# Three of the four column blocks of the embedding's product run at the start, around x's transposes, and wait in DRAM

## The chip, the cores and the metric

One program runs on one core of a Trainium2 chip. The metric is the device time of an execution in microseconds (us); the smaller is the better. The time of a kernel is the median over its runs.

## What is computed

One decoder layer over 512 tokens of width 2048 in float32: RMSNorm, one wide input projection, a recurrence over 16 heads and a pooling group, an output projection with a residual, a gated per-layer embedding, and a final RMSNorm. The change touches the first step and the embedding:

```python
h = rms_norm(x, norm_g[i])
z = jnp.einsum('btd,dn->btn', h, w_in[i])
...
x = x + jnp.einsum('btc,cd->btd', y_mix, w_out[i])
gate = jax.nn.sigmoid(jnp.einsum('btd,de->bte', x, w_pg[i]) + b_pg[i])
x = x + gate * jnp.einsum('btq,qd->btd', p[i], w_ple[i])
return rms_norm(x, final_g)
```

Here p is 512 x 256 and w_ple is 256 x 2048. The product p @ w_ple depends on no other result, so it can run at any time before the gates that use it.

## The kernel before, in words

Every matrix product is made of three: each operand is split into a rounded high part (a cast on ScalarE, ACT) and a low part (a subtraction on VectorE, DVE), and `mm3` (L163) issues high x high, high x low and low x high. A 256 KB piece of weights is loaded on SP's DMA queue into `raw`, then split into `whi` and `wlo` (`wsplit`, L127, or `split`, L136); each of the three has a ring of four buffers.

The stages, in time:

- **Start** (L51 to L298). x comes as four row blocks `xt0` to `xt3` of 128 x 2048, 256 KB or 512 KB at a time. `stats` (L233) squares a block on ACT and DVE, sums, takes the root, and scales the block in place in four quarters. `xt_half(hf, d)` (L264) transposes 128 columns of two row blocks on TensorE (PE) into PSUM; ACT writes the high part `hhi` and DVE the low part `hlo`. There are 2 x 16 such pairs. `z_half` (L274) multiplies them with the 128 columns of the small lora weights (`whi_l`, `wlo_l`) into `zl`. The PSUM tiles of the transposes alternate between the pools `psM` and `psX` of three buffers each. The scheduler may order the matmuls of this stage as it likes.
- **Middle** (L301 to L844). 32 column blocks of w_in for the head groups and 16 for the pooling, pinned in program order on PE; the first is `zk`. The recurrence's small matmuls are threaded between them.
- **Output projection** (L927): four column blocks of 512 of w_out, accumulators `acc_o`, residual x2, transposed back for the gate.
- **Gates** (L1015 to L1042): four column blocks of w_pg, accumulators `acc_g`. `proj` (L877) goes over 16 weight pieces k and, within one, over the four row blocks tt, three matmuls each: 192 matmuls a column block. Accumulators rotate through five PSUM buffers, and a block needs four of them. `gate` (L963) is, for each row block, an addition on DVE that empties the accumulator (L973), a tanh on ACT, two more DVE operations (`gt`), a square on ACT and a multiplication into `x3` on DVE.
- **The embedding** (`embed`, L906): p is transposed and split once, late (L846 to L850). For a column block, two pieces of w_ple pass through the weights' rings, 24 matmuls write four PSUM tiles `pple`, and ACT copies them to `ple`. Block 0 runs in the last block of the output projection (L939). Block ec+1 runs on PE between the projections of gate blocks ec and ec+1 (L1020).

Of the kernel before, what the change touches and what calls it, by code (L numbers as in the profile page):

```python
# [34 lines left out]
def trunk_kernel(ctx: ExitStack, tc: tile.TileContext, x, p, norm_g, w_in, mu, w0, w_up, a0, a_up,  # L35
# [20 lines left out]
    def load_x(tt, parts):  # L56
        xt = xp.tile([P, D], F32, name=f"xt{tt}", tag="xt")
        w_ = D // parts
        for i in range(parts):
            nc.sync.dma_start(out=xt[:, i * w_:(i + 1) * w_], in_=x[tt * P:(tt + 1) * P, i * w_:(i + 1) * w_])  # L60
        xs.append(xt)

    load_x(0, 4)
    ngr = xp.tile([KT, P], F32, name="ngr", bufs=1)
    nc.sync.dma_start(out=ngr, in_=norm_g[0].rearrange("(r c) -> r c", c=P))
# [68 lines left out]
        return hi, lo  # L134

    def split(hi, lo, src):  # L136
        nc.scalar.copy(hi, src)  # L137
        nc.vector.tensor_tensor(lo, src, hi.bitcast(F32), ALU.subtract)  # L138


    def rsqrt(y, v, t):
# [72 lines left out]
    def load_l():  # L214
        n_, c_, src, kt, w_ = plan.pop(0)
        raw = wp.tile([P, kt, w_], F32, name=f"raw_{n_}_{c_}", tag="raw")
        nc.sync.dma_start(out=raw, in_=src)
        lraw.append(raw)

    for step in LORD:  # L220
        if step == "l":
            load_l()
        else:
            load_x(step, 2)

# [2 lines left out]
        nc.sync.dma_start(out=prow[col[n_]:col[n_] + r_, :], in_=flat.rearrange("(r c) -> r c", c=P))  # L228


    WPOS, SPOS = (5, 7, 9, 11), (5, 10)

    def stats(tt, parts=2):  # L233
        w_ = D // parts
        ss = xp.tile([P, parts], F32, name=f"ss{tt}", tag="ss")
        for i in range(parts):
            cs = slice(i * w_, (i + 1) * w_)
            junk = xp.tile([P, w_], F32, name=f"junk{tt}_{i}", tag=f"junk{i % 2}", bufs=2)
            if i % 2 == 0:
                nc.scalar.activation(junk, xs[tt][:, cs], AF.Square, accum_out=ss[:, i:i + 1])  # L240
            else:
                nc.vector.scalar_tensor_tensor(junk, xs[tt][:, cs], 1.0, xs[tt][:, cs], ALU.mult, ALU.mult,
                                               accum_out=ss[:, i:i + 1])
        rs = xp.tile([P, 1], F32, name=f"rs{tt}", tag="rs")
        nc.vector.tensor_reduce(rs, ss, mybir.AxisListType.X, ALU.add)
        nc.scalar.activation(rs, rs, AF.Sqrt, bias=epsr, scale=1.0 / D)
        nc.vector.reciprocal(rs, rs)
        for i in range(4):
            cs = slice(i * D // 4, (i + 1) * D // 4)
            if i % 2 == 1:  # L250
                nc.scalar.activation(xs[tt][:, cs], xs[tt][:, cs], AF.Copy, scale=rs)
            else:
                nc.vector.tensor_scalar(xs[tt][:, cs], xs[tt][:, cs], rs, None, ALU.mult)

    stats(0, 4)
    pt = psM.tile([P, T], F32, name="pt_prm", tag="m")
    nc.tensor.transpose(pt[:, :KT], ngr, ident[:KT, :KT])
# [5 lines left out]

    def xt_half(hf, d):  # L264
        hc = half(hf)
        pt = (psM, psX)[d % 2].tile([P, T], F32, name=f"pt_h{hf}_{d}", tag="mx"[d % 2])
        for i in range(2):
            src = xs[2 * hf + i][:, d * P:(d + 1) * P]
            nc.tensor.transpose(pt[:, i * P:(i + 1) * P], src, ident)
        nc.scalar.activation(hhi[:, d, hc], pt[:, 0:256], AF.Copy, scale=ngc[:, d:d + 1])  # L270
        nc.vector.scalar_tensor_tensor(hlo[:, d, hc], pt[:, 0:256], ngc[:, d:d + 1], hhi[:, d, hc].bitcast(F32),
                                       ALU.mult, ALU.subtract)

    def z_half(hf, d):  # L274
        hc = half(hf)
        wh, wl = wl_[d // CK]
        mm3(zl[:, hc], wh[:, d % CK, :], wl[:, d % CK, :], hhi[:, d, hc], hlo[:, d, hc], d == 0, d == KT - 1)

    wl_ = []
    for d in range(KT):  # L280
        xt_half(0, d)
        if d in WPOS:
            c = len(wl_)
            wh = wp.tile([P, CK, P], F32R, name=f"whi_l_{c}", tag="whi")
            wl = wp.tile([P, CK, P], F32R, name=f"wlo_l_{c}", tag="wlo")
            split(wh, wl, lraw[c])
            wl_.append((wh, wl))
        if d in SPOS:
            stats(2 + SPOS.index(d))
# [5 lines left out]
    pt = psM.tile([P, T], F32, name="pt_prm", tag="m")  # L295
    nc.tensor.transpose(pt[:, :nr], prow, ident[:nr, :nr])
    nc.vector.tensor_copy(prm, pt[:, :nr])
    sx.close()  # L298


# [564 lines left out]
    EC = 512  # L865
    KEEP = 8
    TP = 40
    AS = (3,)
# [37 lines left out]
    def embed(ec, pool):  # L906
        es = slice(ec * EC, (ec + 1) * EC)
        src = w_ple[:, es].rearrange("(k p) n -> p k n", p=P)
        ph, pl = [], []
        for k in range(2):  # L910
            a_, b_ = wsplit(src[:, k:k + 1, :], 1, EC, f"ple{ec}_{k}")
            ph.append(a_)
            pl.append(b_)
        ple = []
        for tt in range(NT):
            ts_ = slice(tt * P, (tt + 1) * P)
            pq = psM.tile([P, EC], F32, name=f"pple{ec}_{tt}", tag="m")
            for k in range(2):
                nc.tensor.matmul(pq, phi[:, k, ts_], ph[k][:, 0, :], start=k == 0, stop=False)  # L919
# [3 lines left out]
            nc.scalar.copy(t_, pq)  # L923
# [25 lines left out]
    with tc.tile_pool(name="fp", bufs=2) as fp, tc.tile_pool(name="kp_", bufs=1) as kp_:  # L949
# [115 lines left out]
```

## Time and profile before

| | |
|---|---|
| median of 3 runs | 1123.04 us (1122.91 to 1123.46) |
| the profiled execution's own time | 1124.35 us |
| its span, first to last instruction | 1122.6 us |
| PE, DVE, ACT, POOL busy | 1081.4, 709.3, 459.9, 75.2 us |
| mean granted TensorE clock | 0.993 |
| DMA | 130.17 MB, mean 116 GB/s |

All times in the trace are from the span's start. PE is TensorE's matmuls, DVE VectorE, ACT ScalarE, POOL GpSimd, SP the queue that issues most loads; PEld is the weight load of PE. A row of a timeline gives start, length, engine, line, operation, what it writes and reads, and in brackets the idle time ahead of it with what ended it. Matmuls are pipelined: a 128x512 one is shown as 0.39 us long, but the next starts 0.23 us behind it, so starts and not lengths are to be subtracted.

### The profile page before, as it was taken

What the parts mean: (1) busy time and instruction counts of PE and PEld (TensorE: products, weight loads), DVE (VectorE), ACT (ScalarE), POOL (GpSimd) and SP (SyncE); (2) the same over time, 40 slices, a digit from 0 to 9 for tenths busy, and PEclk for the clock granted to TensorE, in tenths of its full rate; (3) what the DMA queues carried; (4) which work ended last, traced back from release to release, by engine and by line L of the source; (5) the groups of instructions that cost most, each with busy time, mean ns of one, the idle gap of its engine ahead of it and who ended that gap; (6) DMA issues with size and microseconds to landing.
All of it is one profiled execution on the core that took longest, in us unless ns stands there. A gap on an engine that the chain in (4) does not pass through costs nothing. (4 is left out here: it accounts for less than half of the span.)

```text
span 1122.6 us, 17272 instructions
## 1 busy us (share of the span) xinstructions
PE 1081.4 (96%) x6090; PEld 880.6 (78%) x6090; DVE 709.3 (63%) x1861; ACT 459.9 (41%) x920; POOL 75.2 (7%) x184
## 2 busy tenths in 40 slices
PE   5999999999999998999999999999999999999995
PEld 4888887877877876878778787778888888888885
DVE  6677868778588687687885955564243332525446
ACT  7643536336336353363362343252222232424333
POOL 2100010110110100101101102000000000000001
PEclk9999999999999998999999999999999999999998
DMA  7433332423423332324234233465343444434244
GB/s 228 122 92 96 101 105 69 114 85 82 121 78 93 99 77 71 100 74 110 79 89 120 74 104 96 150 215 174 115 161 125 138 145 155 150 104 151 94 132 150
DMA packets 173877, 130.17 MB, mean 116 GB/s; under 512 B 34165, under 2 KB 139230, under 8 KB 173790
## 3 DMA queue, kind: packets, MB, share of 16 engines
q1 hardware_dynamic: 157694, 103.89, 31.6%
q10 hardware_dynamic: 16096, 25.17, 6.9%
q8 instruction: 48, 0.79, 0.3%
q14 instruction: 39, 0.32, 0.1%
HBM read 113.82 MB, written 14.68 MB: 114 GB/s over the span
## 5 line engine op out<-in xcount | busy, mean ns | idle before, releaser
L133 DVE TENSOR_TENSOR wlo_g<-raw_g,whi_g 128x512 fp32r<-128x512 f32 x88 | 59.4, 684 | 78.6 <-ACT whi_g L132 78.4
L156 PE MATMUL zb<-hhi,whi_b 128*128 128x512 f32 x256 | 107.2, 419 | 0.0
L133 DVE TENSOR_TENSOR wlo_o<-raw_o,whi_o 128x512 fp32r<-128x512 f32 x64 | 43.8, 691 | 93.7 <-ACT whi_o L132 93.7
L156 PE MATMUL acc_o<-wlo_o,yhi 128*128 128x512 f32 x256 | 99.9, 390 | 0.6 <-DVE wlo_o L133 0.6
L156 PE MATMUL zb<-hhi,wlo_b 128*128 128x512 f32 x256 | 100.5, 392 | 0.0
L156 PE MATMUL acc_o<-whi_o,ylo 128*128 128x512 f32 x256 | 100.3, 392 | 0.0
L132 ACT CAST whi_g<-raw_g 128x512 fp32r<-128x512 f32 x88 | 54.3, 623 | 112.2 <-PE acc_g L156 62.1
L156 PE MATMUL zb<-hlo,whi_b 128*128 128x512 f32 x256 | 100.0, 391 | 0.0
L156 PE MATMUL acc_o<-whi_o,yhi 128*128 128x512 f32 x256 | 99.4, 391 | 0.5 <-ACT yhi L137 0.5
L156 PE MATMUL acc_g<-whi_g,x2hi 128*128 128x512 f32 x224 | 86.5, 386 | 0.0
L156 PE MATMUL acc_g<-wlo_g,x2hi 128*128 128x512 f32 x224 | 86.4, 386 | 0.0
L156 PE MATMUL acc_g<-whi_g,x2lo 128*128 128x512 f32 x224 | 86.3, 385 | 0.0
L132 ACT CAST whi_o<-raw_o 128x512 fp32r<-128x512 f32 x64 | 39.7, 623 | 101.1 <-PE acc_o L156 93.6
L749 POOL TENSOR_SCALAR s0p<-sbd,pw 64x64 f32<-64x64 f32 x96 | 52.9, 551 | 331.9 <-DVE sbd L742 255.3
L132 ACT CAST whi_b<-raw_b 128x512 fp32r<-128x512 f32 x64 | 39.6, 619 | 73.5 <-PE zv L156 27.7
L133 DVE TENSOR_TENSOR wlo_b<-raw_b,whi_b 128x512 fp32r<-128x512 f32 x64 | 43.8, 685 | 29.0 <-ACT whi_b L132 28.5
L156 PEld LDWEIGHTS acc_o<-wlo_o,yhi 128*128 128x128 f32 x256 | 48.1, 188 | 11.4 <-DVE wlo_o L133 1.5
L156 PEld LDWEIGHTS zb<-hhi,wlo_b 128*128 128x128 f32 x256 | 48.0, 188 | 10.9
L156 PEld LDWEIGHTS acc_o<-whi_o,yhi 128*128 128x128 f32 x256 | 48.1, 188 | 10.5 <-ACT yhi L137 0.7
L156 PEld LDWEIGHTS acc_o<-whi_o,ylo 128*128 128x128 f32 x256 | 48.1, 188 | 10.0 <-DVE ylo L138 0.4
L597 DVE TENSOR_TENSOR xw<-xw,tm 128x60 f32<-128x60 f32 (+24 forms) x248 | 51.9, 209 | 6.3
L156 PEld LDWEIGHTS zb<-hhi,whi_b 128*128 128x128 f32 x256 | 48.3, 189 | 8.7
(290 smaller groups left out, 2568.2 us busy)
## 6 DMA issues: line engine op xcount, KB each, us to landing
raw_b<-in_w_in_dram SPq DMA_DIRECT2D x64, 256.0 KB
raw_o<-in_w_out_dram SPq DMA_DIRECT2D x64, 256.0 KB
raw_g<-in_w_pg_dram SPq DMA_DIRECT2D x64, 256.0 KB
raw_k<-in_w_in_dram SPq DMA_DIRECT2D x32, 256.0 KB
raw_r<-in_w_in_dram SPq DMA_DIRECT2D x32, 256.0 KB
raw_v<-in_w_in_dram SPq DMA_DIRECT2D x32, 256.0 KB
raw_g<-in_w_in_dram SPq DMA_DIRECT2D x32, 256.0 KB
n<-nd SPq DMA_DIRECT2D x16, 256.0 KB
```

What stands on the lines that cost most here:

```text
L132: nc.scalar.copy(hi, raw)
L133: nc.vector.tensor_tensor(lo, raw, hi.bitcast(F32), ALU.subtract)
L156: i = nc.tensor.matmul(*a, **k)
L597: nc.vector.tensor_tensor(xw[:, 0:n_, s + 1:32], xw[:, 0:n_, s + 1:32], tm[:, 0:n_, 0:w_], ALU.add)
L749: nc.gpsimd.tensor_scalar(s0p[hc, :], nxt[hc, hc], pcn[hc], None, ALU.mult)
```

## The change

Column blocks 1, 2 and 3 of the embedding's product move to the start. A generator `embed_early` transposes and splits p, and hands out the 72 matmuls of the three blocks six at a time; results go from PSUM to a tile `pe_` and on ACT's DMA queue to a DRAM tensor `pled`. `recall` loads a block back from there at the place in the gate stage where `embed(ec + 1)` stood. Block 0 stays where it was, and so do the late transposes and splits of p for it, so p is now loaded and transposed twice.

With it come these:

- SP's queue begins with p (`pn0`, 512 KB) and w_ple's block 1 (`eraw`, 512 KB), ahead of x. Block 2 comes after the first half of x, block 3 after all of x and the lora weights, which now follow x.
- At the start PE is pinned in program order: p's transposes, block 1 (24 matmuls), then the pairs of the first half of x with block 2 between them, then `z_half(0)` with the pairs of the second half four steps behind it, then `z_half(1)`, block 3, and `zk`.
- The low parts of the lora weights and of blocks 2 and 3 are subtracted on POOL (`split_g`); the lora splits come later (WPOS).
- x's transposes use three PSUM buffers (`psX`) and no longer six.

```diff
+    EC = 512
...
+    def load_e(ec):
+        for k in range(2):
+            t_ = xp.tile([P, EC], F32, name=f"eraw{ec}_{k}", tag="eraw", bufs=6)
+            nc.sync.dma_start(out=t_, in_=w_ple[k * P:(k + 1) * P, ec * EC:(ec + 1) * EC])
+            eraw[ec, k] = t_
+
+    load_e(1)
     load_x(0, 4)
...
+    def split_g(hi, lo, src):
         nc.scalar.copy(hi, src)
-        nc.vector.tensor_tensor(lo, src, hi.bitcast(F32), ALU.subtract)
+        nc.gpsimd.tensor_tensor(lo, src, hi.bitcast(F32), ALU.subtract)
...
-    LORD = (2, "l", "l", "l", "l", 3)
+    LORD = ("e2", 2, 3, "l", "l", "l", "l", "e3")
...
-    WPOS, SPOS = (5, 7, 9, 11), (5, 10)
+    WPOS, SPOS = (11, 13, 14, 15), (5, 11)
...
+    def embed_early():
+        ph0 = xp.tile([P, 2, T], F32R, name="ph0", bufs=1)
+        pl0 = xp.tile([P, 2, T], F32R, name="pl0", bufs=1)
+        for k in range(2):
+            pt = psM.tile([P, T], F32, name=f"ppt0_{k}", tag="m")
+            for tt in range(NT):
+                tr(pt[:, tt * P:(tt + 1) * P], pn0[tt // 2][:, tt % 2, k * P:(k + 1) * P], ident)
+            first[:] = split(ph0[:, k, :], pl0[:, k, :], pt)
+        yield 0
+        for ec in range(1, D // EC):
+            w2 = []
+            for k in range(2):
...
+                if ec == 1:
+                    split(hi, lo, eraw[ec, k])
+                else:
+                    with tc.issue_after(ev[0].ins):
+                        split_g(hi, lo, eraw[ec, k])
...
+            for tt in range(NT):
+                ts_ = slice(tt * P, (tt + 1) * P)
+                pq = psM.tile([P, EC], F32, name=f"pe{ec}_{tt}", tag="m")
+                for k in range(2):
+                    hi, lo = w2[k]
+                    mm3(pq, ph0[:, k, ts_], pl0[:, k, ts_], hi, lo, k == 0, k == 1)
+                    yield 3
+                t_ = xp.tile([P, EC], F32, name=f"pe_{ec}_{tt}", tag="pe", bufs=4)
+                if ec == 1:
+                    nc.scalar.copy(t_, pq)
+                else:
+                    nc.vector.tensor_copy(t_, pq)
+                nc.scalar.dma_start(out=pled[ts_, ec * EC:(ec + 1) * EC], in_=t_)
...
+    pin[0] = True
...
+    ple(24)
+    with tc.issue_after(first[0].ins), tc.issue_after(first[1].ins):
+        stats(0, 4)
...
     for d in range(KT):
         xt_half(0, d)
+        ple(2 if d > 3 else 0)
         if d in WPOS:
...
-            split(wh, wl, lraw[c])
+            with tc.issue_after(ev[0].ins):
+                split_g(wh, wl, lraw[c])
...
-    for d in range(KT):
-        xt_half(1, d)
-        z_half(0, d)
+    for d in range(KT + 4):
+        if d >= 4:
+            xt_half(1, d - 4)
+        if d < KT:
+            z_half(0, d)
...
     for d in range(KT):
         z_half(1, d)
...
+    ple(100)
+    pin[0] = False
...
+    def recall(ec, pool):
+        ples[ec] = []
+        for tt in range(NT):
+            t_ = pool.tile([P, EC], F32, name=f"ple{ec}_{tt}", tag="ple", bufs=4)
+            nc.scalar.dma_start(out=t_, in_=pled[tt * P:(tt + 1) * P, ec * EC:(ec + 1) * EC])
+            ples[ec].append(t_)
...
-            embed(ec + 1, fp if ec % 2 == 0 else lp)
+            recall(ec + 1, fp if ec % 2 == 0 else lp)
```

The order of instructions on each engine shows what moved at three places. First, PE at the start, before: after the transpose of norm_g (`ngr`) come the transposes of x (`xt`).

```order
L257 MATMUL pt_prm<-ident,ngr 128x16
L269 MATMUL pt_h_0_198<-ident,xt_78 128x128
L269 MATMUL pt_h_1_203<-ident,xt_78 128x128
L269 MATMUL pt_h_2_208<-ident,xt_78 128x128
L269 MATMUL pt_h_3_213<-ident,xt_78 128x128
```

And PE in the changed kernel from the pair of step 4 on (`pt_h0_4`; `pe2` is block 2, `ehi2` and `elo2` the two parts of w_ple, `ph0` and `pl0` those of p):

```order
L180 MATMUL pt_h0_4_296<-ident_102,xt0_86 128x128
L180 MATMUL pt_h0_4_296<-ident_102,xt1_93 128x128
L176 MATMUL pe2_0_312<-ehi2_0_304,ph0_177 128x512
L176 MATMUL pe2_0_312<-elo2_0_305,ph0_177 128x512
L176 MATMUL pe2_0_312<-ehi2_0_304,pl0_178 128x512
L180 MATMUL pt_h0_5_316<-ident_102,xt0_86 128x128
L180 MATMUL pt_h0_5_316<-ident_102,xt1_93 128x128
L176 MATMUL pe2_0_312<-ehi2_1_308,ph0_177 128x512
L176 MATMUL pe2_0_312<-elo2_1_309,ph0_177 128x512
L176 MATMUL pe2_0_312<-ehi2_1_308,pl0_178 128x512
L180 MATMUL pt_h0_6_337<-ident_102,xt0_86 128x128
```

The pairs of steps 5 and 6 now stand behind products that read POOL's `elo2_0` and `elo2_1`. Ahead of the first `zl` there now stand all 32 transposes of x's first half, the 48 products of blocks 1 and 2 and the transposes of p; before, there were 20 transposes of x and the one of `ngr`.

Second, ACT in the first half of x's splits, with the semaphores that each row waits for. Before:

```order
L246 ACTIVATE rs_237<-rs_237,epsr 128x1 [waits DVE_49]
L137 CAST whi_l_269<-raw_l_144 128x512 [waits DMAHW5_49]
L270 ACTIVATE hhi<-pt_h_10_273,ngc 128x256 [waits PE_49]
L251 ACTIVATE xt_137<-xt_137,rs_237 128x512 [waits DVE_49]
L251 ACTIVATE xt_137<-xt_137,rs_237 128x512 [waits DMAHW2_49]
L240 ACTIVATE junk_0_279,ss_278<-xt_148 128x1024 [waits DMAHW7_49]
```

ACT of the changed kernel there: the store of block 2's first tile stands between the scaling of `xt2` and the tenth split.

```order
L349 ACTIVATE hhi<-pt_h_9_362,ngc 128x256 [waits PE_49]
L273 ACTIVATE xt_149<-xt_149,rs_329 128x512 [waits DVE_49]
L273 ACTIVATE xt_149<-xt_149,rs_329 128x512 [waits DMAHW1_49]
L314 DMA pled<-pe_0_347 128x512 [waits DMAHW6_49,DVE_49]
L349 ACTIVATE hhi<-pt_h_10_367,ngc 128x256 [waits PE_49]
L349 ACTIVATE hhi<-pt_h_11_379,ngc 128x256 [waits PE_49]
L157 CAST whi_l_387<-raw_l_155 128x512
L314 DMA pled<-pe_1_372 128x512 [waits DMAHW7_49,DVE_49]
```

The last DMA on the semaphore DMAHW6 ahead of that store is the small load of a0 on SP (`prow`), which stands behind all the large loads of the start:

```order
L237 DMA raw_l_161<-in_w_in_dram 128x4x128 [waits DMAHW1_49]
L75 DMA eraw_0_163<-in_w_ple_dram 128x512 [waits DMAHW3_49]
L75 DMA eraw_1_165<-in_w_ple_dram 128x512 [waits DMAHW4_49]
L250 DMA prow<-in_mu_dram 25x128 [waits DMAHW5_49]
L250 DMA prow<-in_a_dram 8x128 [waits DMAHW6_49]
```

The DMAs of SP and ACT take eight semaphores in turn, so each waits for the one eight places ahead of it, whichever queue that is on. Before, ACT issued no DMA in this stretch.

Third, PE where gate block 1 begins. Before, the last of the embedding's 24 products (`pple1_3`) and the first of the block:

```order
L919 MATMUL pple1_3_9688<-whi_ple1_1_9657,phi_7807 128x512
L920 MATMUL pple1_3_9688<-wlo_ple1_1_9658,phi_7807 128x512
L921 MATMUL pple1_3_9688<-whi_ple1_1_9657,plo_7808 128x512
L156 MATMUL acc_g1_0_9737<-whi_g1_0_9743,x2hi_7943 128x512
L156 MATMUL acc_g1_0_9737<-wlo_g1_0_9744,x2hi_7943 128x512
L156 MATMUL acc_g1_0_9737<-whi_g1_0_9743,x2lo_7944 128x512
```

PE of the changed kernel there. The products of row block 3 (`acc_g1_3`) stand behind twenty others, since its buffer is the one that the gate of row block 2 empties; before, the 24 products of the embedding stood ahead of all of these.

```order
L176 MATMUL acc_g1_2_9876<-whi_g1_1_9898,x2lo_8121 128x512
L176 MATMUL acc_g1_0_9874<-whi_g1_2_9916,x2hi_8120 128x512
L176 MATMUL acc_g1_0_9874<-wlo_g1_2_9917,x2hi_8120 128x512
L176 MATMUL acc_g1_3_9877<-whi_g1_0_9880,x2hi_8120 128x512
L176 MATMUL acc_g1_3_9877<-wlo_g1_0_9881,x2hi_8120 128x512
L176 MATMUL acc_g1_3_9877<-whi_g1_0_9880,x2lo_8121 128x512
```

The scheduler has moved the products that wait behind those that need not.

More of the change, by code (lines that the diff above doesn't have):

```diff
@@ L61, in load_x @@
         xs.append(xt)
+    EC = 512
+    pn0 = []
+    for h in range(2):
+        t_ = xp.tile([P, 2, DPLE], F32, name=f"pn0_{h}", bufs=1)
+        nc.sync.dma_start(out=t_, in_=p[256 * h:256 * h + 256, :].rearrange("(t p) q -> p t q", p=P))
+        pn0.append(t_)
+    eraw = {}
+    def load_e(ec):
[4 more added lines that the diff above has]
+    load_e(1)
     load_x(0, 4)
@@ L136, in split @@
     def split(hi, lo, src):
+        return nc.scalar.copy(hi, src), nc.vector.tensor_tensor(lo, src, hi.bitcast(F32), ALU.subtract)
+    def split_g(hi, lo, src):
         nc.scalar.copy(hi, src)
-        nc.vector.tensor_tensor(lo, src, hi.bitcast(F32), ALU.subtract)
+        nc.gpsimd.tensor_tensor(lo, src, hi.bitcast(F32), ALU.subtract)
     def rsqrt(y, v, t):
@@ L222, in trunk_kernel @@
             load_l()
+        elif step in ("e2", "e3"):
+            load_e(int(step[1]))
         else:
@@ L256, in trunk_kernel, with ple @@
+    first, ev = [], [None, None]
+    early = embed_early()
+    owed = [0]
+    def ple(n):
+        owed[0] += n
+        while owed[0] > 0:
+            c = next(early, None)
+            if c is None:
+                owed[0] = 0
+                return
+            owed[0] -= c
+    pin[0] = True
+    next(early)
+    next(early)
     pt = psM.tile([P, T], F32, name="pt_prm", tag="m")
-    nc.tensor.transpose(pt[:, :KT], ngr, ident[:KT, :KT])
+    ple(24)
+    with tc.issue_after(first[0].ins), tc.issue_after(first[1].ins):
+        stats(0, 4)
@@ L258, in trunk_kernel @@
+    tr(pt[:, :KT], ngr, ident[:KT, :KT])
     nc.vector.tensor_copy(ngc, pt[:, :KT])
@@ L265, in xt_half @@
         hc = half(hf)
-        pt = (psM, psX)[d % 2].tile([P, T], F32, name=f"pt_h{hf}_{d}", tag="mx"[d % 2])
+        pt = psX.tile([P, T], F32, name=f"pt_h{hf}_{d}", tag="x")
         for i in range(2):
             src = xs[2 * hf + i][:, d * P:(d + 1) * P]
[L269 to L272, printed above, removed]
+            tr(pt[:, i * P:(i + 1) * P], src, ident)
+        ev[0] = nc.scalar.activation(hhi[:, d, hc], pt[:, 0:256], AF.Copy, scale=ngc[:, d:d + 1])
+        ev[1] = nc.vector.scalar_tensor_tensor(hlo[:, d, hc], pt[:, 0:256], ngc[:, d:d + 1], hhi[:, d, hc].bitcast(F32),
+                                               ALU.mult, ALU.subtract)
     def z_half(hf, d):
@@ L864, in trunk_kernel @@
     x2d = dram.tile([T, D], F32, name="x2d", bufs=1)
-    EC = 512
     KEEP = 8
```

16 lines of the change are left out of this document (11 added, 5 removed).

## Prediction

> **What bounds the kernel now.** I first read the page, then the windows by stage, then the chain of waits, then the timelines of the start and of one boundary between gate blocks. The page gives the span and the engines' busy time:
>
> ```profile
> span 1122.6 us, 17272 instructions
> PE 1081.4 (96%) x6090; PEld 880.6 (78%) x6090; DVE 709.3 (63%) x1861; ACT 459.9 (41%) x920; POOL 75.2 (7%) x184
> ```
>
> PE is busy 96% of the span. The windows show where it is not (start, length, busy time and count of each engine, granted clock, DMA share, GB/s):
>
> ```profile
> 0.00:12.00 12.00, 2.03 (x7) 1.18 (x7) 4.76 (x17) 6.17 (x15) 6.48 (x54) 1.00 0.79 259
> 12.00:26.00 14.00, 12.37 (x74) 10.55 (x75) 12.80 (x32) 13.77 (x32) 0.00 (x0) 1.00 0.74 225
> 26.00:36.00 10.00, 9.94 (x85) 9.68 (x84) 9.27 (x23) 8.21 (x21) 0.00 (x0) 1.00 0.11 30
> 36.00:1094.00 1058.00, 1040.06 (x5832) 844.41 (x5831) 663.44 (x1732) 421.26 (x832) 64.14 (x126) 1.00 0.38 113
> 1094.00:1122.00 28.00, 17.04 (x98) 14.74 (x96) 19.01 (x60) 10.46 (x23) 4.62 (x4) 0.85 0.42 151
> 2.00:18.00 16.00, 7.39 (x30) 5.71 (x31) 9.92 (x28) 10.98 (x28) 5.22 (x44) 1.00 1.01 322
> ```
>
> PE stands idle for 10 us of the first 12, while x arrives. From 2 to 18 us the DMA engines are full (share 1.01) at 322 GB/s. From 12 to 26 us ACT is busy 13.77 of 14.00 us: that half of the transposes goes at ACT's pace, and PE's 74 matmuls in it count as busy partly because their modelled ends wait for one another. From 36 to 1094 us PE is the bound. So whatever delays the first matmul of that stretch (`zk`) moves the end by the same amount, and a matmul taken out of the stretch moves it back by the same amount. The chain of waits confirms it for the late part (start, length, what):
>
> ```profile
> 968.56 43.52 PE acc_g L156 x192
> 1017.52 43.52 PE acc_g L156 x192
> 1094.29 0.70 DVE gt L973
> ```
>
> **What is taken away.** From one gate block to the next it is 1017.52 - 968.56 = 48.96 us, for 192 + 24 matmuls on PE: 0.2267 each, so 24 cost 5.44. Three such groups go: **-16.3 us**. ACT's copies from `pple` to `ple` go with them, and DRAM loads come in their place in a stretch where the DMA share is 0.38; their 3 MB lie beside PE's work, and I cost them at nothing. Were one of them late, the gate's last multiplication would wait, which is not in PE's way.
>
> But the 24 matmuls also covered something. At a boundary:
>
> ```profile
> 962.96 0.39 PE L919 MATMUL pple<-whi_ple,phi 128*128 128x512 f32 x1
> ...
> 961.71 1.28 DVE L973 TENSOR_TENSOR gt<-acc_g,bB 128x512 f32<-128x512 f32 x2
> 966.71 1.28 DVE L973 TENSOR_TENSOR gt<-acc_g,bB 128x512 f32<-128x512 f32 x2
> ```
>
> The old block's last matmul ends about where `pple` begins, 962.96. DVE empties accumulators 0 and 1 from 961.71, does other parts of the gates, and empties 2 and 3 from 966.71: the third buffer is free at 967.35, that is 4.4 us after the block's end. The next block has one spare buffer and two early ones; its fourth accumulator needs the third of the old ones. In plain program order it would be wanted after 9 matmuls, 2.0 us, and PE would stall 2.4 us at each of three boundaries (7.2). The new order puts twenty matmuls there, 20 x 0.2267 = 4.5 us, which just covers 4.4. I take 0.1 each, **+0.3** (0 to 7.2).
>
> **What is added at the start.** Three stages follow one another. The rows are of PE, DVE and ACT there; the last two are groups, ACT's copies of `pple` and POOL's only tensor operations of this shape with their mean in ns:
>
> ```profile
> 12.45 1.54 PE L269 MATMUL pt_h<-ident,xt 128*128 128x128 f32 x6 [1.64 <-DVE xt L253]
> 17.65 0.41 PE L156 MATMUL zl<-hhi,whi_l 128*128 128x256 f32 x1
> 17.87 0.33 PE L156 MATMUL zl<-hlo,whi_l 128*128 128x256 f32 x1
> 18.03 0.28 PE L156 MATMUL zl<-hhi,wlo_l 128*128 128x256 f32 x1
> 18.15 0.28 PE L156 MATMUL zl<-hhi,whi_l 128*128 128x256 f32 x1
> 27.15 0.38 PE L269 MATMUL pt_h<-ident,xt 128*128 128x128 f32 x2
> 27.61 0.38 PE L269 MATMUL pt_h<-ident,xt 128*128 128x128 f32 x2
> 35.70 0.48 PE L156 MATMUL zk<-hhi,whi_k 128*128 128x512 f32 x1
> ...
> 10.39 0.69 DVE L242 SCALAR_TENSOR_TENSOR junk<-xt 128x512 f32<-128x512 f32 x1 [0.38 <-DMA xt<-in_x_dram]
> 26.10 7.22 DVE L271 SCALAR_TENSOR_TENSOR hlo<-pt_h,ngc,hhi 128x256 fp32r<-128x256 f32 x18
> ...
> 15.29 0.64 ACT L137 CAST whi_l<-raw_l 128x512 fp32r<-128x512 f32 x1
> 15.80 1.09 ACT L240 ACTIVATE junk<-xt 128x1024 f32<-128x1024 f32 x1
> 19.87 1.39 ACT L251 ACTIVATE xt<-xt,rs 128x512 f32<-128x512 f32 x2
> 26.29 4.85 ACT L270 ACTIVATE hhi<-pt_h,ngc 128x256 fp32r<-128x256 f32 x13
> ...
> L923 ACT COPY ple<-pple x16: 567/588/590, 913.7 to 1066.7; 128x512 f32<-128x512 f32 x16
> ...
> L981 POOL TENSOR_TENSOR x<-gt,gB 128x512 f32<-128x512 f32 x3 | 3.9, 1297 | 408.1 <-DVE gt L978 408.1
> ```
>
> *x later.* p and block 1 of w_ple, 1.05 MB, go ahead of x: 1.05 MB / 322 GB/s = +3.3 us. The last piece of block x1 is used at 10.39, the first pairs are transposed at 12.45. In that gap ACT also has copies of block 1 to make, 0.59 each by the group of copies; two of them in the path are +1.2. The first pairs start at 12.45 + 4.5 = 16.95. Block 1's 24 products and p's transposes fit into PE's idle time ahead of it and cost nothing there.
>
> *First half.* Before, ACT's splits of the first half end at 26.29, where those of the second begin. Carried 4.5 later, and lengthened by:
> - two casts of block 2's weights on ACT, 0.51 each (15.29 to 15.80): +1.0;
> - POOL: the pairs of steps 5 and 6 stand behind products of `elo2_0` and `elo2_1`. Two subtractions take 2 x 1.30, in a time in which ACT has a square of 1.09 to do anyway: +1.5 (0 to 2.6);
> - a semaphore. ACT's store of block 2's first tile waits for the one that SP's load of a0 carries, and that load stands behind 7.3 MB of loads on SP; with 1.05 MB of stores of block 1 on the same engines that is 8.4 MB, at 322 GB/s from 2.0 us on not before 28.1. ACT comes there at 19.87 + 1.39 = 21.26, plus 4.5, 1.0 and 1.5, less 1.5 for three lora casts that now come later: 26.8. Behind the store, in ACT's order, stand the splits from the eleventh on, and PE's transposes wait for those. About 1.3, with the landing itself 1.5 (0 to 4.5);
> - three PSUM buffers for transposes in place of six: 0.5 (0 to 1.5).
>
> Block 2's 24 products lie between the pairs while ACT sets the pace, and cost nothing. First half: 26.29 + 4.5 + 1.0 + 1.5 + 1.5 + 0.5 = 35.3.
>
> *Second half, and what now stands ahead of `zk`.* Before, products of `zl` ran in both halves. Now all wait for it. A step with two transposes and two `zl` took 27.61 - 27.15 = 0.46; with the third, 0.12 more (18.15 - 18.03), 0.58. Twelve such steps are 6.96. Four at DVE's pace, 7.22 / 18 = 0.40, are 1.6. Then 48 products of `zl` for the second half at 0.12, 5.76, and block 3's 24, 5.44. Together 19.8: `zk` at 55.1. For a cold array I add 0.5 (0 to 2.5): the first two `zl` came 0.22 apart (17.65 to 17.87), two later ones 0.12. `zk` at 55.6, against 35.70: **+19.9**.
>
> On that last point the rows say that matmuls around 17.9 us go at about half pace while the granted clock in the windows stands at 1.00 there, so that column doesn't show it. The Trainium skill, "TensorE: Matmul & The Clock Gate", Part 1, gives the half clock as the array's default state, released by some 3.4 us of sustained activity and set again by an idle window; the trace roughly agrees on the ratio (0.22 to 0.12). By its 426.7 ns for a cold matmul of 512 columns, 24 products would cost 24 x (0.427 - 0.227) = 4.8 us more (an estimate); it speaks against early work between pauses.
>
> **The sum.** -16.3 + 0.3 + 19.9 = **+3.9 us**: the span of 1122.6 becomes 1126.5. The profiled execution's own time was 1124.35, the median 1123.04; I add the difference to the median: **1126.9 us**. 0.2%, 2.2 us, is about what a measurement of this kernel can tell from no change.
>
> **Rivals.**
> - *Faster: the start packs well.* No wait for POOL, the semaphore or PSUM (-3.5), no copies in x's path (-1.2), no cold array or stall at boundaries (-0.8), and the second half at DVE's pace throughout, 16 x 0.40 = 6.4 for 8.56 (-2.2). That is 7.7 less: 1119.2. Its place is the first matmul of `zk`: the delay must stay under 16.3 - 2.2 = 14.1, so `zk` before 49.8. For it: 10 idle us of PE at the start. Against it: that ACT, not PE, sets the first half's pace, and gets more work there. 0.15.
> - *No change: the waits on POOL, semaphore and PSUM don't come* (-3.5), the rest does: 1123.4. For it: ACT has other work by which a late operand may be hidden. 0.23.
> - *Slower still.* Either each of block 2's four stores waits for another of SP's small loads, 1.5 each, so 3 x 1.5 = 4.5 more, 1131.4; or the array cools between pairs, and block 2's products take 0.22 / 0.12 of their warm time, 0.227 x 0.83 = 0.19 more each, 24 x 0.19 = 4.6, 1131.5. Against it: the small loads land one behind another, and ACT's own pace hides some. 0.16.
> - That the change doesn't do what it says is excluded by the order: the 72 products stand at the start and none between the gate blocks.
>
> The forecast itself has 0.46.
>
> **How the numbers follow.** Low end: the forecast without its unknown costs, POOL 1.5, semaphore 1.5, PSUM 0.5, copies 1.2, cold array 0.5, boundaries 0.3, which is 5.5 less: 1121.4. High end: the worse of the two slower cases, 1131.5 rounded up to 1132.0. Outside lie most of the faster case and the tails of the slower one, about 0.2. Faster 0.15, same 0.23, slower 0.46 + 0.16 = 0.62.
>
> **What would show it.** Right: `zk` begins between 53 and 58 us; the first pair of x near 17; ACT idle at the store of block 2's first tile, with a DMA as releaser; PE idle at `elo2` with POOL as releaser; three `acc_g` blocks of 43.5 us that follow one another without a gap. Wrong: `zk` before 50, or gaps of over 2 us at the boundaries of gate blocks, or a lower clock there; then the sum fails at its start or at its boundary term.

## The result and the profile after

The changed kernel takes 1135.28 us (1133.98 to 1135.73), the kernel before 1123.25 us beside it: ratio 1.0104 (95% interval 1.0087 to 1.0122), 12.0 us slower. The direction was forecast and the size was not: 1126.9 was predicted, 1132.0 was the upper end.

The page of the changed kernel, its first two lines, answers to that of before: the span is 11.4 us longer, and PE's share is the same.

```profile
span 1134.0 us, 17331 instructions
PE 1087.8 (96%) x6098; PEld 884.4 (78%) x6098; DVE 714.0 (63%) x1863; ACT 458.7 (40%) x914; POOL 84.3 (7%) x192
```

The windows of the changed kernel by stage (same columns as before):

```profile
17.50:25.40 7.90, 2.24 (x12) 1.20 (x11) 3.34 (x9) 4.83 (x12) 0.00 (x0) 0.74 1.05 370
25.40:31.50 6.10, 5.50 (x15) 4.06 (x16) 2.46 (x7) 2.92 (x6) 2.50 (x2) 0.50 0.51 174
31.50:41.80 10.30, 7.04 (x41) 5.25 (x40) 8.94 (x20) 7.58 (x17) 1.30 (x1) 1.00 0.32 103
41.80:45.00 3.20, 3.20 (x18) 3.18 (x16) 1.66 (x4) 2.64 (x7) 3.09 (x3) 0.50 0.18 51
60.00:1100.00 1040.00, 1022.47 (x5756) 830.58 (x5755) 657.86 (x1717) 410.31 (x812) 63.47 (x126) 1.00 0.40 117
```

Two things are new. From 17.5 to 25.4 us PE has 12 matmuls in 7.9 us, and neither ACT (4.83) nor DVE (3.34) is full. From 25.4 to 31.5, and again from 41.8 to 45.0, the granted clock stands at 0.50; before, no window of the start showed less than 1.00.

At the late end all is as forecast. The chain of waits shows the gate blocks as one piece without a gap, where before it had three of 43 us with a group of `pple` between them:

```profile
947.57 135.30 PE acc_g L176 x598
```

So the loss is at the start. PE's timeline there, from the first transposes of x to `zk`:

```profile
17.61 0.33 PE L180 MATMUL pt_h<-ident,xt 128*128 128x128 f32 x1
18.96 0.77 PE L180 MATMUL pt_h<-ident,xt 128*128 128x128 f32 x5 [1.02 <-DVE xt L275]
20.82 1.04 PE L180 MATMUL pt_h<-ident,xt 128*128 128x128 f32 x4 [1.09 <-DVE hlo L350]
25.45 0.80 PE L176 MATMUL pe<-ehi,ph 128*128 128x512 f32 x1 [3.59 <-ACT ehi L157]
26.80 0.79 PE L176 MATMUL pe<-elo,ph 128*128 128x512 f32 x1 [0.56 <-POOL elo L158]
27.39 0.63 PE L176 MATMUL pe<-ehi,pl 128*128 128x512 f32 x1
27.82 0.63 PE L180 MATMUL pt_h<-ident,xt 128*128 128x128 f32 x2
...
40.48 0.41 PE L180 MATMUL pt_h<-ident,xt 128*128 128x128 f32 x2 [2.35 <-DVE hlo L350]
...
63.95 0.39 PE L176 MATMUL zk<-hhi,whi_k 128*128 128x512 f32 x1
```

`zk` begins at 63.95 and not at 55.6. The row at 17.61 is a transpose of x's first row block alone; the second row block, with which a pair is complete, follows at 18.96, in the place of the row at 12.45 before. PE stands still for 3.59 us ahead of block 2's first product and waits for ACT's cast of `ehi`; after it, what follows a product starts 0.43 us behind it (27.39 to 27.82), nearly twice 0.2267. ACT's timeline in the same stretch (rows of ACTq are DMA issues):

```profile
15.40 0.36 ACTq L314 DMA_DIRECT2D pled<-pe  x1
...
19.79 1.19 ACT L349 ACTIVATE hhi<-pt_h,ngc 128x256 fp32r<-128x256 f32 x3
23.68 0.33 ACTq L314 DMA_DIRECT2D pled<-pe  x1
24.05 0.84 ACT L349 ACTIVATE hhi<-pt_h,ngc 128x256 fp32r<-128x256 f32 x2 [3.07 <-DMA pled<-pe]
24.78 1.14 ACT L157 CAST ehi<-eraw 128x512 fp32r<-128x512 f32 x2
28.48 0.47 ACT L349 ACTIVATE hhi<-pt_h,ngc 128x256 fp32r<-128x256 f32 x1 [2.57 <-PE pt_h L180]
...
43.49 0.47 ACT L349 ACTIVATE hhi<-pt_h,ngc 128x256 fp32r<-128x256 f32 x1
```

ACT is held for 3.07 us at a store, as the prediction had it, but at the fourth store of block 1 and not at the first of block 2. The order says why: it waits for the same semaphore as block 1's second store.

```
L314 DMA pled<-pe_1_219 128x512 [waits DMAHW2_49,Activation_49]
L314 DMA pled<-pe_3_301 128x512 [waits DMAHW2_49,Activation_49]
```

That one was issued at 15.40, and the fourth went out at 23.68, 8.3 us later: the store lay on DMA engines whose share was 1.05. Behind the store stood two splits and ACT's casts of block 2's weights, behind the casts PE's products, behind these, in the pinned order, the next pair of x, and for that pair ACT waited in turn, 2.57 us. The row at 19.79 is x's first split, the last one the first split of x's second half; the forecast had 35.3 there. Before, the second half began at 26.29, and x's first split was this:

```profile
13.15 2.28 ACT L270 ACTIVATE hhi<-pt_h,ngc 128x256 fp32r<-128x256 f32 x6
```

So the delay of 28.2 us at `zk` falls into three stages. x's first split is 6.6 us later; from there to the second half it takes 23.7 us and no longer 13.1; from there to `zk` 20.5 and no longer 9.4.

### The profile page after: what moved, and what is told of

Read it like the earlier page. It is cut to its first block, busy times and chain, and to the rows that moved or that the text cites. A ratio compares the mean times of both kernels' runs of the same rounds, so it can differ in the third digit from the quotient of the medians.

```text
span 1134.0 us, 17331 instructions
## 1 busy us (share of the span) xinstructions
PE 1087.8 (96%) x6098; PEld 884.4 (78%) x6098; DVE 714.0 (63%) x1863; ACT 458.7 (40%) x914; POOL 84.3 (7%) x192
## 3 DMA queue, kind: packets, MB, share of 16 engines
q1 hardware_dynamic: 158238, 104.42, 31.5%
## 5 line engine op out<-in xcount | busy, mean ns | idle before, releaser
L176 PE MATMUL acc_g<-whi_g,x2hi 128*128 128x512 f32 (+1 forms) x224 | 86.8, 388 | 0.0
L176 PE MATMUL acc_g<-wlo_g,x2hi 128*128 128x512 f32 (+1 forms) x224 | 86.5, 386 | 0.0
L176 PEld LDWEIGHTS acc_o<-wlo_o,yhi 128*128 128x128 f32 x256 | 48.1, 188 | 11.2 <-DVE wlo_o L149 1.3
L176 PEld LDWEIGHTS zb<-hhi,wlo_b 128*128 128x128 f32 x256 | 48.1, 188 | 10.9
```

The lines of the kernel that those rows point to most:

```text
L176: i = nc.tensor.matmul(*a, **k)
```

## The experiments

The theory after the result: three waits at the start, the store, the half clock and POOL, account for what the forecast missed; the late part is as worked out. The rival: the first half is bound by something that lies behind all three, and taking one away moves little. Each time stands against runs of the kernel before on the same chip; the changed kernel against its own is at +12.0 us. The intervals reach some 1.7 us to each side, so two versions whose times differ by less than about 2.4 us are not told apart by them. `zk`, the start of its first matmul, is read from one profiled execution of each; in late_only, which starts as the kernel before does, it is 0.3 us off.

**late_only**: is the saving real, and do the boundaries hold? In the kernel before:

```diff
-            embed(ec + 1, fp if ec % 2 == 0 else lp)
+            recall(ec + 1, fp if ec % 2 == 0 else lp)   # reads rows of x
```

> The kernel before without the three late blocks of products: in their place the gates read rows of x from DRAM, so the embedding's blocks 1 to 3 are not computed at all. Theory (matmuls taken out of the PE-bound stretch save their own time, and the new order covers the boundaries): 72 x 0.2267 = 16.3 us less, 1123.2 - 16.3 = 1106.9, between 1106.3 and 1107.8, with zk still at 35.7 us. Rival (the products covered the wait for the accumulators): 2.4 us back at each of three boundaries, 1114.1.

1106.49 us beside 1122.60, ratio 0.9852 (0.9836 to 0.9869): 16.1 us less, with `zk` in place:

```profile
35.99 0.48 PE L156 MATMUL zk<-hhi,whi_k 128*128 128x512 f32 x1
...
918.92 135.29 PE acc_g L156 x598
```

The saving and the cover at the boundaries are confirmed, and all of the 28.2 us by which `zk` is later come from the start.

**stores_late**: the store's wait. In the changed kernel, tiles `pe_` get eight buffers, and

```diff
-                nc.scalar.dma_start(out=pled[ts_, ec * EC:(ec + 1) * EC], in_=t_)
+                held.append((ec, ts_, t_))      # block 3: stored at once
...
+    for ec, ts_, t_ in held:                    # behind the last split of x
+        with tc.issue_after(ev[0].ins):
+            nc.scalar.dma_start(out=pled[ts_, ec * EC:(ec + 1) * EC], in_=t_)
```

> The changed kernel with the stores of blocks 1 and 2 issued behind the last split of x, none of them between ACT's splits. Theory (ACT stood behind the fourth store of block 1, which waited for the landing of the second on a full DMA): the stall of 3.1 us goes and all that follows moves up by it, zk from 63.95 to between 59.5 and 61, 1135.3 - 3.1 = 1132.2, or down to 1131 if the loads come earlier too. Rival (the casts and products behind the store would have waited anyway, for their own loads or for PE): less than 1 us, 1134.5 to 1135.3.

1129.93 beside 1122.60, ratio 1.0066 (1.0051 to 1.0081): +7.3 where the changed kernel has +12.0. `zk` is 5.5 us earlier, more than the 3.1 of the stall:

```profile
58.45 0.39 PE L176 MATMUL zk<-hhi,whi_k 128*128 128x512 f32 x1
```

ACT's first split of x:

```profile
18.02 1.18 ACT L352 ACTIVATE hhi<-pt_h,ngc 128x256 fp32r<-128x256 f32 x3
```

It comes 1.8 us earlier than the 19.79 of the changed kernel, so 3.7 of the 5.5 are gained behind it. How much of the 1.8 is the stores' is open: in the later pinned versions with the stores late and the same opening (late_dve, late_dve_warm, casts_early) this split lies between 18.6 and 19.1. The store is the largest of the missed costs. Here the waits of block 2 and the half clock (0.50 from 21 to 27 us) remain.

**lo_on_dve**: POOL.

```diff
-        nc.gpsimd.tensor_tensor(lo, src, hi.bitcast(F32), ALU.subtract)
+        nc.vector.tensor_tensor(lo, src, hi.bitcast(F32), ALU.subtract)
```

> The changed kernel with the low parts of blocks 2, 3 and of the lora weights subtracted on DVE and no longer on POOL. Theory (POOL's 1.3 us each hold PE up by 0.6 at the first product, and hold DVE's square of x3 up by 1.1): 1.5 to 2.4 us less, 1133 to 1133.8; the square of x3 on DVE back at 1.2 us. Rival (DVE's own queue gets as much longer): no change, or up to 4 x 0.64 = 2.6 more, 1137.9.

1132.81, ratio 1.0090 (1.0075 to 1.0105): +10.2, 1.8 us less than the changed kernel, with `zk` 1.9 us earlier (62.00). The square of x3 on DVE, first of the changed kernel, then of this one:

```profile
36.33 2.28 DVE L264 SCALAR_TENSOR_TENSOR junk<-xt 128x1024 f32<-128x1024 f32 x1
```

```profile
36.34 1.22 DVE L264 SCALAR_TENSOR_TENSOR junk<-xt 128x1024 f32<-128x1024 f32 x1
```

While POOL subtracted from 36.24 on, DVE's instruction took 1.06 us longer. The Trainium skill, "GPSIMD Engine Reference", section 1, says that POOL shares its SBUF interfaces with VectorE, in contention with DVE instructions that have two SBUF inputs. This square reads x twice, and the trace agrees. PE's wait of 0.56 for `elo` goes as well; what each of the two gave alone was not tried.

**warm**: the half clock. Ahead of block 2's products:

```diff
+            if ec == 2:
+                pd = psA.tile([P, EC], F32, name="pd", tag="acc")
+                for i in range(14):
+                    mm(pd, ph0[:, 0, 0:P], w1[0][0], start=True, stop=True)
```

> The changed kernel with 14 further matmuls on PE in front of block 2's products, where PE stood idle from 21.8 to 25.4 us; their result is not used. Theory (PE's idle time ahead of block 2 halves its clock for 6.1 us, which then sets the pace): granted clock near 1.00 from 25.4 to 31.5, and 2 to 3 us less, 1132.3 to 1133.3. Rival (ACT's splits set the pace there and hide PE's): the clock rises, the time doesn't move by more than 0.7: 1134.6 to 1136. If the clock stays at 0.5, the run tells nothing of the price.

1132.23, ratio 1.0087 (1.0072 to 1.0102): +9.6, 2.4 us less, with 14 matmuls more. The same two windows:

```profile
25.40:31.50 6.10, 5.67 (x29) 3.82 (x27) 3.59 (x10) 3.82 (x10) 2.11 (x2) 1.00 0.37 130
41.80:45.00 3.20, 3.20 (x30) 3.20 (x29) 2.74 (x7) 2.60 (x6) 1.56 (x2) 1.00 0.72 230
```

The clock is back at 1.00, and 29 matmuls fit where 15 did. `zk` is 3.2 us earlier (60.75); 0.6 of that is there already at x's first split (19.20), ahead of the further matmuls, and 2.6 come behind it. So the slow products were on the path, and ACT's pace did not hide them.

What brought the clock down is not settled, and it was not the pause. In the changed kernel the column's mean of 0.74 over the 7.9 us from 17.5 means that it fell to 0.50 at about 21.3, while PE's pause began at 21.86 (20.82 + 1.04); from 17.61 on PE had done transposes with two waits of about 1 us. The second stretch, from 41.8, came over a microsecond behind the end of a wait of 2.35. And in block1_only (below), where PE's longest wait in this half is 1.8 us, the column stands at 0.50 from about 18.4 past 30, while PE does hardly anything but transposes:

```profile
18.00:24.00 6.00, 3.83 (x16) 2.43 (x16) 4.95 (x13) 5.49 (x15) 0.00 (x0) 0.53 0.80 228
24.00:30.00 6.00, 3.49 (x14) 1.96 (x13) 5.28 (x13) 6.00 (x14) 0.00 (x0) 0.50 0.16 46
```

A lightly loaded PE was enough, without a long pause; whether the load counts there or the kind of matmul was not tried.

**late_dve** and **late_dve_warm**: do these costs add up? First stores late and low parts on DVE, then with 8 of the unused matmuls as well.

> The changed kernel with both edits: stores of blocks 1 and 2 behind x's splits, and the low parts on DVE. Theory (two separate costs): 5.4 + 2.0 less than the changed kernel, zk near 56.5 us, 1127.0 to 1128.0. Rival (both edits remove the same wait): no better than the better of the two, 1129 to 1130.

> The same with 8 further matmuls on PE ahead of block 2's products, whose result is not used, to keep its clock up. Theory (store, POOL and cold clock together are what the forecast's sum had too small): zk between 54 and 55.6, 1125.3 to 1127, which is about the forecast. Rival (with the gap gone the clock is up without them, or ACT sets the pace): the same as without the 8 matmuls within 0.7, or worse by up to 1.8 if they stand in the way.

1129.53 beside 1122.96, ratio 1.0066 (1.0051 to 1.0081), +6.6; and 1127.15, ratio 1.0044 (1.0028 to 1.0059), +4.2. The rows of `zk`:

```profile
58.60 0.39 PE L176 MATMUL zk<-hhi,whi_k 128*128 128x512 f32 x1
```

```profile
55.86 0.39 PE L176 MATMUL zk<-hhi,whi_k 128*128 128x512 f32 x1
```

The first missed its range: with the stores out of the way DVE in place of POOL gives 0.7 us in time and nothing at `zk`, within what runs differ; x's first split is 1.1 us later here than in stores_late (19.10), so from that split on it gives 0.9. The second lands where the prediction had put the changed kernel, `zk` 55.6 and 1126.9. The three waits together are 8.1 us at `zk`; singly they had given 5.5, 1.9 and 3.2, 10.6 in sum. Counted from x's first split, which itself shifts between runs, they are 7.0 together and 3.7, 1.7 and 2.6 singly, 8.0 in sum, so they overlap by about 1.

**loads_first**: what do bytes ahead of x cost? The kernel before, with p and block 1 of w_ple loaded ahead of x and not used.

```diff
+        nc.sync.dma_start(out=t_, in_=p[256 * h:256 * h + 256, :].rearrange("(t p) q -> p t q", p=P))
...
+        nc.sync.dma_start(out=t_, in_=w_ple[k * P:(k + 1) * P, 512:1024])
     load_x(0, 4)
```

> The kernel before with the loads of p and of block 1 of w_ple ahead of x on SP's queue, and nothing done with them. Theory (x comes later by the bytes ahead of it): 1.05 MB / 322 GB/s = 3.3 us, zk at 39.0, 1125.9, between 1125.3 and 1126.8. Rival (the first half of x's splits is bound by ACT and takes a later x up): less than 1.5 us, below 1124.2.

1127.12, ratio 1.0046 (1.0029 to 1.0063): +4.2, above the forecast range. In the timeline of this run, then in the windows:

```profile
40.39 0.48 PE L162 MATMUL zk<-hhi,whi_k 128*128 128x512 f32 x1
```

```profile
2.00:18.00 16.00, 2.66 (x11) 2.18 (x12) 5.25 (x18) 6.18 (x17) 4.87 (x44) 1.00 0.89 277
```

The DMA moved 277 GB/s from 2 to 18 us, and 1.05 MB at that rate are 3.8; at 322 they were 3.3. The term was 1 us too small, and it alone takes back most of a block's 5.4. All of it lies ahead of x's first split; the stages behind take as long as before.

**x_first**: x's first two blocks ahead of p and w_ple, and blocks 1 and 2 between the pairs of the first half (with stores late and low parts on DVE, w_ple's block 2 loaded behind x2, and the copies out of PSUM shared between ACT and DVE).

```diff
-    load_e(1)
     load_x(0, 4)
...
     load_x(1, 4)
+    # p, then load_e(1)
...
-        ple(2 if d > 3 else 0)
+        if d == 2:
+            next(early)
+        ple(4 if d > 3 else 0)
```

> The changed kernel with both edits (stores late, low parts on DVE), and x's first two row blocks loaded ahead of p and w_ple; blocks 1 and 2 both run between the transposes of x's first half. Theory (what must precede x on the DMA engines and on ACT is what the early work costs; PE has idle time between the transposes): first pair back near 12.5 us, zk between 49.5 and 53, 1120 to 1124.3. Rival (ACT and DVE are full in the first half, so that 16 further casts, subtractions and copies of some 0.6 us each, on two engines, take all of it back): zk at 55 or later, 1126 or more.

1129.70, ratio 1.0064 (1.0044 to 1.0083), +6.7, and `zk` at 59.94: the rival's number. ACT's waits from 12 to 50 us (what is waited for, us in total, times, longest):

```profile
ACT pe L310 <- PE pe L176: 5.9, 3, 2.9
ACT hhi L347 <- PE pt_h L180: 1.3, 3, 0.5
```

But it was not work that was too much: ACT waited for PE for over 7 us, and PE for ACT's casts 2.8. I formed another theory: the casts stand in ACT's queue behind the splits that empty PE's stock of pairs, so PE and ACT take turns.

**casts_early** and **x_first_casts**: the casts of a block's weights placed four pairs or so earlier, first with p ahead of x, then with x first.

```diff
     for d in range(KT):
         xt_half(0, d)
+        if d == 1:                 # x first: block 1 at d == 0, block 2 at d == 5
+            next(early)            # block 2's casts
         ple(2 if d > 3 else 0)
```

> The changed kernel with stores late and low parts on DVE, and the casts of block 2's weights placed behind the split of x's second pair, no longer the fifth, those of block 3 inside the second half of x. Theory (PE waits for a cast that ACT reaches only when it has no pair of x left, and then ACT waits for PE, which runs at half clock from the pause: the two alternate): PE goes from the fifth pair straight into block 2, zk from 58.6 to between 54 and 55.5, 1124.5 to 1126.5. Rival (ACT and DVE have too much work in the first half, whatever its order): zk above 57.5, 1128.5 or more.

> The same with x's first two row blocks ahead of p and w_ple on SP's queue, p's transposes just ahead of x's, the casts of block 1 behind the first pair's split and those of block 2 behind the sixth's; blocks 1 and 2 run between the pairs of x's first half. Theory (alternation of PE and ACT, not their total work, was what cost the earlier kernel with x first its time): zk between 50 and 54, 1120.5 to 1125. Rival (total work of ACT and DVE): zk at 57 or later, 1127.5 or more.

1126.58 beside 1122.26, ratio 1.0037 (1.0023 to 1.0052), +4.3, against +6.6 without; and 1126.27, ratio 1.0034 (1.0022 to 1.0047), +4.0, against +6.7. `zk` is at 56.64 in both, between the two theories: 2.0 and 3.3 us earlier. But the clock moved along with the order. From 24 to 30 us, in late_dve, casts_early and late_dve_warm:

```profile
24.00:30.00 6.00, 6.00 (x25) 4.69 (x23) 3.56 (x9) 3.81 (x9) 0.00 (x0) 0.65 0.34 107
```

```profile
24.00:30.00 6.00, 5.12 (x31) 4.06 (x30) 5.62 (x14) 5.17 (x13) 0.00 (x0) 0.98 0.21 69
```

```profile
24.00:30.00 6.00, 5.21 (x31) 3.75 (x30) 6.00 (x16) 5.54 (x13) 0.00 (x0) 1.00 0.31 96
```

In x_first the clock is at 0.73 from 30 to 36 us, in x_first_casts at 1.00. And late_dve_warm, with its casts left late and the clock kept up, gained as much as casts_early (`zk` 55.86). So the gain of 2 to 3 us is shown; that it is the price of taking turns, apart from that of the clock, is not. What remains in the second shows in a window of it:

```profile
24.00:36.00 12.00, 11.97 (x71) 9.76 (x70) 11.63 (x29) 11.50 (x27) 0.00 (x0) 1.00 0.19 54
```

From 24 to 36 us PE, DVE and ACT are all full. There the rival is right: 16 further instructions of some 0.6 us on ACT and DVE have no room left in the first half.

**block1_only**: block 1 early, 2 and 3 late as before, in the changed kernel's form (stores late, low parts on DVE).

> Only block 1 runs early (stores late, low parts on DVE, p and block 1 ahead of x as in the changed kernel); blocks 2 and 3 run between the gate blocks as before. It gives 5.4 us back late. Theory (what costs is the later x, the copies on ACT and the pinned order with all of the lora product behind x's first half; the other two blocks cost about the 10.9 they save): zk near 48.5, 1129 to 1131. Rival (each block costs alike): a third of the 6.6 us that all three lose in this form, 1125.2.

1130.06, ratio 1.0065 (1.0049 to 1.0081): +7.8, no better than all three blocks in this form, +6.6. `zk` is at 46.87, so the other two blocks move `zk` by 11.7 (to 58.60) and save 10.9. All of the loss sits in what comes with the first block. By stages, `zk` is 11.2 us later because x's first split is 4.9 later (18.05), the first half 1.4 longer, and the way from the second half to `zk` 14.3 us in place of 9.4: no lora product runs in x's first half, and all of them follow. Less the 5.4 saved, that would be 5.8; the 2.0 us more in the measured time stay open.

**unpinned**: casts_early with PE's order at the start left to the scheduler (without `pin[0] = True`).

> The changed kernel with stores late, low parts on DVE and casts early, and PE's order at the start left to the scheduler. Theory (the pinned order moves nothing but lora products, which PE has to do anyway before zk): within 0.7 us of the pinned one, 1126 to 1127.3. Rival (pinning it costs what the order of the kernel before hid): zk 2 us or more earlier than 56.6, 1124.5 or less.

1126.20 beside 1122.82, ratio 1.0030 (1.0017 to 1.0042), +3.4. `zk` begins at 53.42, 3.2 us earlier, as the rival had it, but the time is 0.9 less. This decides little: between `zk` and the first gate block some of the gain was lost again, and the clock stays at 1.00 from 16 to 40 us here, so that the earlier `zk` may be the clock's.

**block1_free** and **block1_x_first**: what is left if only what fits is moved. The kernel before, its order free, with block 1 alone early; p and w_ple come behind x's first two row blocks, or still later; results are stored behind x's splits.

```diff
-    LORD = (2, "l", "l", "l", "l", 3)
+    LORD = ("p", "e", 2, "l", "l", "l", "l", 3)    # or (2, "l", "l", "p", "e", "l", "l", 3)
...
         xt_half(0, d)
+        if d == 1: turn_p()                        # or 5
+        if d == 2: cast_e()                        # or 7
+        if d in (4, 6, 8, 10): prod(...)           # or (9, 11, 13, 15)
```

> The same with p and block 1 ahead of x's third row block, that is behind x's first two, and products from the fifth pair on. Theory (the same work, earlier): like the other within 1 us, 1120.5 to 1122. Rival (the casts of the lora weights and the third row block's sum, which come 3.3 us later, hold up the first half): 1123 or more.

> The kernel before with block 1 alone run early: p and block 1 of w_ple are loaded behind x's first three row blocks and two pieces of the lora weights, its products may go wherever the scheduler puts them in x's first half, the results are stored behind x's splits and recalled at the gate; blocks 2 and 3 run where they did. It saves 5.4 us late. Theory (what fits into PE's idle time without delaying x is free but for ACT's and DVE's work, 4 casts, 4 subtractions and 4 copies of some 0.6 us on two engines, 3.6 us): zk at 39 to 40, delay 3.3 to 4.3, 1 to 2 us less than before, 1120.5 to 1121.5. Rival (x3 comes 3.3 us later and holds up the second half too): zk at 41 or later, no change or slower, 1122.5 or more.

block1_free takes 1120.38 us beside 1122.82, ratio 0.9980 (0.9970 to 0.9989): 2.4 us less than the kernel before, and the only version that computes all and beats it. `zk` is 3.6 us later, nearly all of it in the first half (16.7 us in place of 13.1), and 5.4 are saved:

```profile
39.32 0.48 PE L156 MATMUL zk<-hhi,whi_k 128*128 128x512 f32 x1
```

block1_x_first takes 1125.32, ratio 1.0022 (1.0013 to 1.0031), with `zk` at 44.41: slower, although it does the same work. x is not what is late: the second half's first split stands at the same place in block1_free and here,

```profile
30.12 4.12 ACT L311 ACTIVATE hhi<-pt_h,ngc 128x256 fp32r<-128x256 f32 x11 [0.17 <-PE pt_h L310]
```

```profile
30.18 0.47 ACT L311 ACTIVATE hhi<-pt_h,ngc 128x256 fp32r<-128x256 f32 x1
```

but from there to `zk` it is 9.2 us in the one and 14.2 in the other. Its first lora product comes at 29.63 us, that of block1_free at 23.72: what block 1's products push out of the first half has to be done in the second, as in block1_only. The expectation had these two about equal, and the better one turned out to be the one with the loads close behind x1.

## Why the prediction missed, point by point

- **Late part: right.** -16.3 forecast, -16.1 measured alone (late_only), and no gap at the boundaries (0.3 forecast).
- **x later: too small by 2.1.** The first pair was forecast for 16.95, 4.5 behind the row at 12.45; the same row stands at 18.96, and x's first split is 6.6 us later. The last piece of x1 is used at 14.88, 4.5 behind the 10.39 of before, where 3.3 was forecast for the bytes; loads_first alone cost 4.2 in time. From there to the first pair it takes 4.1 us in place of 2.1, so the copies and stores on ACT cost 2.0 and not 1.2.

```profile
14.88 0.69 DVE L264 SCALAR_TENSOR_TENSOR junk<-xt 128x512 f32<-128x512 f32 x1 [0.94 <-DMA xt<-in_x_dram]
```

- **First half: the step that failed.** "First half: 26.29 + 4.5 + 1.0 + 1.5 + 1.5 + 0.5 = 35.3" came out as 43.49. From x's first split on, the half took 10.6 us longer than before, where 4.5 was forecast (1.0 + 1.5 + 1.5 + 0.5): 6.1 of the miss of 8.4 at `zk`. The terms for the waits were too small:
  - The semaphore's mechanism was right, its place and size were not. I had worked out when SP's loads land, and had left out that ACT's own stores take the same eight semaphores in turn and land late on full DMA engines. It was priced at 1.5, at most 4.5; with the stores out of the way `zk` came 5.5 earlier, 3.7 of it behind x's first split (stores_late).
  - "For a cold array I add 0.5" measured 2.4 in time and 3.2 at `zk`, 2.6 of it behind x's first split (warm). The rival that I gave with 4.6 us had it: the array cooled, and block 2's products ran at 0.50 for 6.1 us. By the Trainium skill, "TensorE: Matmul & The Clock Gate", Part 1, an idle window of about 3.4 us sets the half clock. The trace has a pause of 3.59, but the clock fell about half a microsecond ahead of it, and in block1_only without any wait above 1.8, so a lightly loaded PE was enough here, and that rule alone does not give it. I had assumed that ACT's pace hides slow products, and a pinned order doesn't let it.
  - POOL's 1.5 was about right alone (1.8, lo_on_dve), but DVE's square of x3, 1.06 us longer, was a way that I had not priced.
  - The 0.5 for three PSUM buffers in place of six was taken apart by no run. From 12 to 45 us PE waits 4.3 us for DVE's `hlo`, the last reader of a buffer, in the changed kernel (the 1.09 and the 2.35 above among them), 2.5 in late_dve_warm, and 0.8 before; how much of this six buffers would have saved is open.
- **"Block 2's 24 products lie between the pairs while ACT sets the pace, and cost nothing": wrong.** With products and pairs in one pinned queue on PE, and splits and casts in one on ACT, PE and ACT waited for each other (3.59 and 2.57 us). Casts four pairs earlier gave 2.3 us back (casts_early), with the clock's share in it not separated.
- **Second half: right.** 19.8 and 0.5 forecast; from 43.49 to 63.95 it is 20.5.

Without the three waits (late_dve_warm) `zk` is 8.1 us earlier than in the changed kernel, about the 8.4 of the miss. That it then meets the forecast is luck: the forecast had already held 3.5 us for them, so some 3.7 us of that kernel's delay come from elsewhere in the start. By stages, about 1.1 of these lie ahead of x's first split (18.71), 1.8 in the first half (16.4 us) and 0.9 behind it (20.7 us). The first is x's loads and copies; for the 1.8, casts that stand late on ACT and the three PSUM buffers are the candidates, and they were not taken apart; the 0.9 stays open.

## What to carry to other kernels

Idle time of one engine at the start is worth only what can be fed to it: count the bytes ahead of the first input and the casts and copies on the engines that set the pace, and move no more than fits (here one block of three, with its loads behind the first input). Work that the moved part pushes out of that idle time comes back in full later, as the 5 us of lora products did. An in-order queue must not hold a store ahead of work on the path while the DMA engines are full, and a cast is better placed ahead of the point where its consumer runs out of other work. A stretch in which PE mostly waits is paid twice, once in the waits and once in the clock after it.

## What the runs showed that I had not expected

- At the very start of the changed kernel block 1's products are 0.43 us apart, as at half clock, while the granted clock of that window reads 1.00; so the column doesn't show the first slow stretch, only the later ones. Rows of PE's timeline and of the windows:

```profile
11.27 0.63 PE L176 MATMUL pe<-elo,ph 128*128 128x512 f32 x1
11.70 0.63 PE L176 MATMUL pe<-ehi,pl 128*128 128x512 f32 x1
```

```profile
9.00:14.30 5.30, 5.03 (x12) 3.68 (x13) 3.87 (x11) 3.85 (x10) 0.00 (x0) 1.00 1.02 329
```

- A delay of `zk` reaches the end only within some 3 us. From `zk` to the first gate block it was 884.6 us before (920.25 - 35.70), 883.6 in the changed kernel, 881.2 in casts_early and 884.1 in unpinned. In late_only, the same as before up to there, it was 882.9, so 1.6 of this is what runs differ; in unpinned `zk` was 3.2 us earlier than in casts_early, and the time 0.4 less (0.9 against its own runs of before). Why was not tried.
